# An encoder layer on one core: input loads one step later, grouped exponentials, weight sums at half rate, four buffers for values

## The chip, the core and the metric

The kernel runs on one core of one Trainium2 chip. The metric is the device time of one execution in microseconds (us); the kernel before has a median of 2715.44 us over three runs (2715.1 to 2720.17).

The engines are TensorE (PE in the profile, its weight loads PEld), VectorE (DVE), ScalarE (ACT), GpSimd (POOL) and SyncE (SP). SP, ACT and POOL also issue DMAs. Each engine works through its own instructions in order: an instruction that waits holds all that stand behind it, and an instruction that issues a DMA waits like any other.

## The reference

One bidirectional encoder layer with shared weights on 256 + 1024 tokens of width 1024, all in float32. Cut to the parts that this case touches:

```python
h = rmsnorm(x, g_mix_pre)
z = h @ w_in
rq, rk, rv, rg, pin, mq, gl = jnp.split(z, list(IN_SPLITS), axis=-1)
gates = jax.nn.sigmoid(gl).reshape(b, s, N_BRANCH, D_MODEL)
# retention: scores times a decay matrix exp(log_gamma * distance), per head
decay = jnp.where(mask[None], jnp.exp(log_gamma[:, None, None] * jnp.maximum(diff, 0.0)[None]), 0.0)
y_ret = retention_branch(rq, rk, rv, rg, decay_fwd, decay_bwd, ret_gn) @ w_ret_out
# pooling: four groups of 256 channels, windows 2, 4, 8, 16
mean = (csg[:, hi] - csg[:, lo]) / (hi - lo)[None, :, None]
outs.append(mean - pf[:, :, sl])          # then a 256x256 product per group
y_pool = pool_branch(pin, pool_w, pool_scale) @ w_pool_out
# memory attention: keys and values from a normalised memory
kv = rmsnorm(mem, g_mem) @ w_mem_kv
y_mem = memory_branch(mq, mem, g_mem, w_mem_kv) @ w_mem_out
merged = gates[:, :, 0] * y_ret + gates[:, :, 1] * y_pool + gates[:, :, 2] * y_mem
x = x + rmsnorm(merged @ w_o, g_mix_post)
x = x + rmsnorm(conv_ffn(rmsnorm(x, g_ffn_pre), w_up, conv_w, conv_b, w_down), g_ffn_post)
```

## The kernel before

Every product is made of three matmuls of rounded halves (mm3): operands are split into a high part by ACT and a rest by DVE (hilo, and split_to for weights). Weights come as units of 128 x 1024: SP loads a unit into one of two raw buffers wr, ACT makes wh, DVE makes wl, into a ring of four; a raw buffer is loaded again when its split is issued, and a ring slot is free when PE is done with the unit four before. The order of all instructions on all engines is that of the Python code (a manual schedule). Small background generators in the list bg are advanced by one step at each call of tick(), after the weight split and the sum steps of that tick.

The stages in order, with the steps that the change touches:

- Memory keys: eight units m, each 24 matmuls; from m = 4 on DVE scales two finished banks per unit into tiles st (pool st0, three buffers) which POOL stores to km. In the background x_stats normalises x (loads by POOL, squares on ACT, scaling and hilo of eight hT tiles).
- Memory values: token_major with four weight units held and four token tiles in four PSUM banks (mm), twice (p = 0, 1). After the last unit mem_v evicts each bank on ACT into a tile st of the same three buffers, and ACT issues its store to vm.
- Value projection: token_major over ten token tiles, in blocks of 4, 1, 1 and 4 tiles, twice; v_out evicts into vst (two buffers) and ACT stores to vd. There are ten ticks per half. In the background in_terms loads eight chunks xs of x transposed on ACT's queue (three buffers), scales them on DVE and writes the sums and differences T1 to T4, two hilo's a step.
- Quads: twelve groups of four weight units (u0, s12, s34, a2), 7-product scheme; s12 and s34 are sums of weights that were formed in DRAM.
- Keys with rotary, memory attention, gates, then pooling and decay tables, states, retention, merge, output and the MLP. The MLP uses 22 more quads with formed sums.

The sums are made by DMA alone: sums() gives, for each of 34 quads, five steps: two plain copies issued by ACT (step 0) and four accumulating DMAs issued by POOL (steps 1 to 4), each on what an earlier step wrote. Step i of quad q is given out in round q + lag * i. sum_step() takes one step; tick() takes adding[0] of them: 1 in the memory values, 2 in the value projection, 1 later; each release of a weight unit in the quads takes one too. A load of s12 or s34 whose sum is not finished in this order takes all missing steps first.

pool_chain runs in the background of nine gate units (27 ticks). Per window: split the 256x256 weights into pwh, then for each of two channel tiles add shifted copies of an input tile pin on DVE, subtract, hilo into dh (one tick each), one empty tick, then two ticks of products evicted by ACT into ypo (two buffers), which POOL stores. load(m) takes a pin buffer, clears three edges with POOL memsets and loads two pieces on SP's queue. decay_matrix runs beside it and does one head per tick: two DVE operations, an Exp on ACT, a scaling on DVE. The gates use Sigmoid on ACT in between.

Of the kernel before, what the change touches and what calls it, by code (L numbers as in the profile page):

```python
# [17 lines left out]
P = 128  # L18
D = 1024
TP = 256  # L20
# [104 lines left out]
def encoder(ctx: ExitStack, tc: tile.TileContext, a: dict):  # L125
# [75 lines left out]
    summed = set()  # L201

    def sums():
        lag = 2

        def stage(i, q):
            u, v = (r.rearrange("p (a b) -> p a b", b=512) for r in sum_rows[q])
            both = lambda x: x.unsqueeze(1).to_broadcast([P, 2, 512])
            s12, s34 = s12_d[q], s34_d[q]
            if i == 0:  # L210
                nc.scalar.dma_start(out=s12[:], in_=both(v[:, 0, :]))
                nc.scalar.dma_start(out=s34[:], in_=u)
            elif i == 1:
                nc.gpsimd.dma_start(out=s12[:], in_=both(v[:, 1, :]), accum_op=ALU.add)
            elif i == 2:
                nc.gpsimd.dma_start(out=s34[:, 0, :], in_=v[:, 0, :], accum_op=ALU.add)
            elif i == 3:
                nc.gpsimd.dma_start(out=s12[:, 1, :], in_=u[:, 0, :], accum_op=ALU.add)
            else:
                nc.gpsimd.dma_start(out=s34[:, 1, :], in_=s12[:, 1, :], accum_op=ALU.add)  # L220
                summed.add(q)

        for n in range(len(sum_rows) + 4 * lag):
            for i in range(5):
                q = n - lag * i
                if 0 <= q < len(sum_rows):
                    stage(i, q)
                    yield
# [232 lines left out]
    def decay_matrix(pool):  # L461
        rel = pool.tile([P, 2, 2 * C], F32, name="rel")
        nc.sync.dma_start(out=rel, in_=a["rel"])
        yield
        for h in range(H):
            dt = dtab[:, h].rearrange("p a b -> p (a b)")
            nc.vector.tensor_scalar(out=dt, in0=rel[:, 0, :], scalar1=lg[:, h:h + 1], scalar2=None, op0=ALU.mult)
            nc.vector.scalar_tensor_tensor(out=dt, in0=rel[:, 1, :], scalar=lg[:, H + h:H + h + 1], in1=dt,
                                           op0=ALU.mult, op1=ALU.add)
            nc.scalar.activation(dt, dt, AF.Exp)  # L470
            nc.vector.tensor_scalar(out=dt, in0=dt, scalar1=HD ** -0.5, scalar2=None, op0=ALU.mult)
            yield

    def token_major(base, lhs, nt, out):
        blocks = [range(4)] if nt == 4 else [range(4), (4,), (5,), range(6, nt)]
# [19 lines left out]
    bg.append(mem_stats())  # L495
    bg.append(x_stats())
    bg.append(decay_tables())
    with tc.tile_pool(name="st0", bufs=3) as stp:
        done = []
        for m in range(8):  # L500
            (wh, wl), = ws.take()
# [16 lines left out]
                done = done[2:]  # L518
            tick()
        def mem_v(p, j, b):  # L520
            o = stp.tile([P, TM], F32, tag="st", name="st")
            nc.scalar.activation(o, b, AF.Copy, scale=mrs[:, j:j + 1])
            nc.scalar.dma_start(out=vm_d[p][:, j], in_=o[:].rearrange("p (a b) -> p a b", b=HD))

# [52 lines left out]

    def in_terms(pool):
        def load(c):
            t = pool.tile([P, TS], F32, tag="xs", name="xs", bufs=3)  # L580
            nc.scalar.dma_start(out=t, in_=a["xT"][:, c, TP:T])
            return t

# [4 lines left out]
        def put(nm, c, r):  # L588
            hilo(r, in_term(nm, c, 0), in_term(nm, c, 1))

        r1, r2 = load(0), load(4)
        yield
        for c in range(4):
            scaled(r1, c)
            if c < 3:
                n1 = load(c + 1)
            yield
            scaled(r2, c + 4)
            mix(r1[:, LO], r1[:, LO], r1[:, HI])
            put("T1", c, r1[:, LO])  # L600
# [4 lines left out]
            put("T2", c, r2[:, HI])  # L605
            mix(r2[:, LO], r2[:, HI], r2[:, LO], -1.0)
            put("T4", c, r2[:, LO])
            if c < 3:
                r1, r2 = n1, load(c + 5)
            yield  # L610

    with tc.tile_pool(name="vproj", bufs=1) as vp:
        def v_out(p, t, b):
            o = vp.tile([P, 512], F32, tag="vst", name="vst", bufs=2)
            nc.scalar.activation(o, b, AF.Copy)
            nc.scalar.dma_start(out=v_d[p][:, t], in_=o[:].rearrange("p (a b) -> p a b", b=HD))

        bg.append(in_terms(vp))
        adding[0] = 2
        token_major(v_at, hT, NT, v_out)  # L620
        drain()
    adding[0] = 1
# [2 lines left out]
    with tc.tile_pool(name="quads", bufs=1) as qp:  # L625
# [74 lines left out]
        for q in range(NQ):  # L700
            d, more = Q[q], q + 1 < NQ
            product(d["a"], unit("s12", q, 1), "T2", False, True)
            u2 = snap(qtile("u2", 2)[:], d["a"])
            pr(q, 0, 1)
            d["d"] = mmb(512)
            product(d["d"], unit("s34", q, 0), "T3", True, True)
            product(d["a"], unit("s12", q, 0), "T1", False, True)
# [194 lines left out]

    def pool_chain():
        pieces = ((PAD, 0, TP), (PAD + TP + PAD, TP, TS))
        pin = {}

        def load(m):
            if m < 2 * len(WINDOWS):
                t = pin[m] = pp.tile([P, PWA], F32, tag="pin", name="pin", bufs=2)
                for s in (0, PAD + TP, PW - PAD):  # L910
                    nc.gpsimd.memset(t[:, s:s + PAD], 0.0)
                for s, o, n in pieces:
                    nc.sync.dma_start(out=t[:, s:s + n], in_=pin_d[m // 2][:, m % 2, o:o + n])

# [11 lines left out]
        for g, w in enumerate(WINDOWS):  # L926
# [2 lines left out]
            load_w(g + 1)  # L929
            dh = []  # L930
            for c in range(2):
                x = pin.pop(2 * g + c)
                cur, lo, hi = x, PAD - 8, PW - PAD + 7
                step = 1
                while step < w:
# [25 lines left out]
                t = pp.tile([P, 2, PWA], F32R, tag="dh", name="dh", bufs=2)[:, :, 0:PCOLS]  # L961
                hilo(r, t[:, 0], t[:, 1])
                dh.append(t)
                load(2 * g + c + 2)
                yield
            yield
            for e in range(2):
                es = slice(e * P, (e + 1) * P)
# [986 lines left out]
```

## Time and profile before

| | |
|---|---|
| median of 3 runs | 2715.44 us |
| profiled execution | 2714.67 us |
| its span | 2712.9 us |
| PE busy | 2622.4 us (97%) |
| DVE, ACT, POOL busy | 1415.7, 982.7, 335.4 us |
| DMA, mean rate | 171 GB/s |

Busy time is the time in which an engine has an instruction running. What matters for the time is where PE has none: the list of waits gives for each engine and line the engine, tile and line that ended the wait, the sum in us, the count and the longest. In a timeline a row has start, duration, engine (ACTq and SPq are DMA issues), line, operation, output<-input and in brackets the idle time just before it and what ended it. The chain of waits is the list of work that ended last, followed back from the end.

### The profile page before, as it was taken

How to read it: one execution, taken by the hardware profiler on the slowest of the kernel's cores; microseconds unless marked ns; L12 is line 12 of the kernel's file. 1: busy time of each engine (PE TensorE's matmuls, PEld its weight loads, DVE VectorE, ACT ScalarE, POOL GpSimd, SP SyncE). 2: the span in 40 equal slices, each digit the busy share in tenths (PEclk: the TensorE clock that was granted, in tenths of full speed). 3: DMA queues.
4: the chain of work that ended last, by engine and by line, in shares of the span. 5: the costliest groups of instructions: out<-in, count | busy, mean ns of one | idle time of the engine just before them, and what ended most of it. 6: DMA issues, size and time to landing. Idle time of an engine off the chain costs nothing.

```text
span 2712.9 us, 35194 instructions
## 1 busy us (share of the span) xinstructions
PE 2622.4 (97%) x13580; PEld 2240.8 (83%) x13580; DVE 1415.7 (52%) x2343; ACT 982.7 (36%) x1637; POOL 335.4 (12%) x525
## 2 busy tenths in 40 slices
PE   8879999999988999999999999998999999999998
PEld 6668888889976788889888888877888888888886
DVE  4532323456624366688732444557666655664554
ACT  5322323324432233333321220466444444444443
POOL 1121222222222222111100000010000000000000
PEclk9889999999988999999999999999999999999999
DMA  7998777787667687555443442452333333354343
GB/s 270 310 267 223 209 213 217 211 245 196 186 165 213 170 225 205 191 177 185 147 170 121 132 148 88 159 194 88 112 111 113 113 108 115 113 183 153 143 158 109
DMA packets 181433, 464.88 MB, mean 171 GB/s; under 512 B 20721, under 2 KB 48241, under 8 KB 180721
## 3 DMA queue, kind: packets, MB, share of 16 engines
q1 hardware_dynamic: 111072, 268.33, 29.5%
q0 software_dynamic: 54384, 146.83, 21.0%
q10 hardware_dynamic: 15808, 47.47, 5.3%
q8 instruction: 106, 1.74, 0.2%
q14 instruction: 63, 0.51, 0.1%
HBM read 360.58 MB, written 182.19 MB: 200 GB/s over the span
## 4 chain that ended last, share of the span: by engine, by line
PE 83%; DMA 6%; DVE 5%; ACT 3%; issue 2%; POOL 0%; SPq 0%; ACTq 0%; DVEq 0%; POOLq 0%
PE f L1521 15%; PE f L164 10%; PE f L163 10%; PE f L162 10%; PE mm L639 7%; PE mm L162 6%; PE mm L163 6%; PE mm L164 6%; PE ch L163 3%; PE ch L164 3%; PE ch L162 3%; PE ch L639 1%; DMA wr<-w_kv_in 1%; DMA vm<-st 1%; DMA vd<-vst 1%
## 5 line engine op out<-in xcount | busy, mean ns | idle before, releaser
L90 DVE TENSOR_TENSOR wl<-wr,wh 128x1024 fp32r<-128x1024 f32 x268 | 327.5, 1224 | 516.1 <-ACT wh L89 511.2
L89 ACT ACTIVATE wh<-wr 128x1024 fp32r<-128x1024 f32 x268 | 280.7, 1051 | 269.1 <-PE f L163 150.6
L162 PE MATMUL mm<-b,wh 128*128 128x512 f32 (+1 forms) x960 | 342.6, 357 | 0.0
L163 PE MATMUL mm<-b,wh 128*128 128x512 f32 (+1 forms) x960 | 341.1, 355 | 0.0
L164 PE MATMUL mm<-b,wl 128*128 128x512 f32 (+1 forms) x960 | 340.5, 355 | 0.0
L1521 PE MATMUL f<-b,wh 128*128 128x512 f32 x880 | 273.8, 392 | 0.0
L164 PEld LDWEIGHTS mm<-b,wl 128*128 128x128 f32 x960 | 182.2, 190 | 25.7
L162 PEld LDWEIGHTS mm<-b,wh 128*128 128x128 f32 x960 | 182.5, 190 | 24.2
L163 PEld LDWEIGHTS mm<-b,wh 128*128 128x128 f32 x960 | 182.5, 190 | 23.6
L1521 PEld LDWEIGHTS f<-b,wh 128*128 128x128 f32 x880 | 162.0, 189 | 30.7
L1521 PE MATMUL f<-b,wl 128*128 128x512 f32 x440 | 171.9, 391 | 0.0
L163 PE MATMUL f<-b,wh 128*128 128x512 f32 (+1 forms) x432 | 153.4, 355 | 0.0
L162 PE MATMUL f<-b,wh 128*128 128x512 f32 (+1 forms) x432 | 153.1, 355 | 0.0
L164 PE MATMUL f<-b,wl 128*128 128x512 f32 (+1 forms) x432 | 152.8, 354 | 0.0
L164 PE MATMUL f<-wh,gl 128*128 128x512 f32 x390 | 151.8, 389 | 0.1
L162 PE MATMUL f<-wh,gl 128*128 128x512 f32 x390 | 151.8, 389 | 0.0
L163 PE MATMUL f<-wl,gl 128*128 128x512 f32 x390 | 151.7, 389 | 0.0
L155 DVE TENSOR_TENSOR gl<-b,gl 128x640 fp32r<-128x640 f32 x78 | 64.3, 825 | 118.2 <-ACT gl L154 116.9
L639 PE MATMUL mm<-T,wh 128*128 128x512 f32 x384 | 118.9, 391 | 0.5 <-ACT q L568 0.5
L154 ACT ACTIVATE gl<-b 128x640 fp32r<-128x640 f32 x78 | 57.5, 740 | 153.8 <-PE f L164 153.8
L1521 PE MATMUL f<-hc,wh 128*128 128x512 f32 x352 | 108.9, 391 | 0.0
L162 PE MATMUL f<-h2p,wh 128*128 128x256 f32 x352 | 100.0, 284 | 3.2 <-ACT h2p L154 3.2
(383 smaller groups left out, 5940.8 us busy)
## 6 DMA issues: line engine op xcount, KB each, us to landing
wr<-w_in_in SPq DMA_DIRECT2D x72, 512.0 KB, 5.3
wr<-w_up_in SPq DMA_DIRECT2D x44, 512.0 KB, 3.5
wr<-w_down_in SPq DMA_DIRECT2D x44, 512.0 KB, 3.5
wr<-s12d SPq DMA_DIRECT2D x34, 512.0 KB, 3.6
wr<-s34d SPq DMA_DIRECT2D x34, 512.0 KB, 3.5
b<-fgd SPq DMA_DIRECT2D x44, 320.0 KB, 5.2
h2s<-gtd SPq DMA_DIRECT2D x48, 256.0 KB, 3.7
s12d<-w_up_in ACTq DMA_DIRECT2D x22, 512.0 KB, 5.7
```

Source lines behind the costliest of these rows:

```text
L89: self.nc.scalar.activation(h, r[:], AF.Copy)
L90: self.nc.vector.tensor_tensor(out=l, in0=r[:], in1=h.bitcast(F32), op=ALU.subtract)
L154: nc.scalar.activation(hi, src, AF.Copy)
L155: nc.vector.tensor_tensor(out=lo, in0=src, in1=hi.bitcast(F32), op=ALU.subtract)
L162: nc.tensor.matmul(out, ah, bh, start=first, stop=False)
L163: nc.tensor.matmul(out, ah, bl, start=False, stop=False)
L164: nc.tensor.matmul(out, al, bh, start=False, stop=last)
L639: nc.tensor.matmul(b, w[x][:, ks], in_term(nm, c, y), start=first and c == k == 0, stop=last and c == 3 and k == 2, skip_group_check=True)
L1521: nc.tensor.matmul(b, w[x][:, ks], hterm(nm, c, y), start=first and c == k == 0, stop=last and c == 3 and k == 2, skip_group_check=True)
```

## The change

- sums(): lag is 1 instead of 2, so the five steps of a quad lie in consecutive rounds.
- The value projection takes one sum step per tick instead of two; each quad takes one more (five instead of four).
- decay_matrix: the heads' first two DVE operations still take one tick each, but all four Exps come in one tick after them, and all four scalings in the next.
- Pool st0: the tiles st for km have two buffers; mem_v uses tiles sv with four buffers of their own.
- in_terms: xs has two buffers instead of three; both loads of a chunk stand at the start of its turn, and the work starts two ticks later; a chunk takes four ticks instead of three.
- vst has four buffers instead of two.
- pool_chain: two lasting tiles pin0 and pin1, whose edges are cleared once at the start; a tile's next load is issued one tick later.

```diff
 def sums():
-        lag = 2
+        lag = 1
@@ decay_matrix
+        dt = [dtab[:, h].rearrange("p a b -> p (a b)") for h in range(H)]
         for h in range(H):
-            dt = dtab[:, h].rearrange("p a b -> p (a b)")
-            nc.vector.tensor_scalar(out=dt, in0=rel[:, 0, :], scalar1=lg[:, h:h + 1], ...)
-            nc.vector.scalar_tensor_tensor(out=dt, in0=rel[:, 1, :], scalar=lg[:, H + h:H + h + 1], in1=dt, ...)
-            nc.scalar.activation(dt, dt, AF.Exp)
-            nc.vector.tensor_scalar(out=dt, in0=dt, scalar1=HD ** -0.5, scalar2=None, op0=ALU.mult)
+            nc.vector.tensor_scalar(out=dt[h], in0=rel[:, 0, :], scalar1=lg[:, h:h + 1], ...)
+            nc.vector.scalar_tensor_tensor(out=dt[h], in0=rel[:, 1, :], scalar=lg[:, H + h:H + h + 1], in1=dt[h], ...)
             yield
+        for h in range(H):
+            nc.scalar.activation(dt[h], dt[h], AF.Exp)
+        yield
+        for h in range(H):
+            nc.vector.tensor_scalar(out=dt[h], in0=dt[h], scalar1=HD ** -0.5, scalar2=None, op0=ALU.mult)
@@ memory keys and values
-    with tc.tile_pool(name="st0", bufs=3) as stp:
+    with tc.tile_pool(name="st0", bufs=2) as stp:
...
         def mem_v(p, j, b):
-            o = stp.tile([P, TM], F32, tag="st", name="st")
+            o = stp.tile([P, TM], F32, tag="sv", name="sv", bufs=4)
@@ in_terms
-            t = pool.tile([P, TS], F32, tag="xs", name="xs", bufs=3)
+            t = pool.tile([P, TS], F32, tag="xs", name="xs", bufs=2)
...
-        r1, r2 = load(0), load(4)
-        yield
         for c in range(4):
+            r1, r2 = load(c), load(c + 4)
+            yield
+            yield
             scaled(r1, c)
-            if c < 3:
-                n1 = load(c + 1)
-            yield
             scaled(r2, c + 4)
...
-            if c < 3:
-                r1, r2 = n1, load(c + 5)
             yield
@@ value projection
-            o = vp.tile([P, 512], F32, tag="vst", name="vst", bufs=2)
+            o = vp.tile([P, 512], F32, tag="vst", name="vst", bufs=4)
...
-        adding[0] = 2
@@ quads
             pr(q, 0, 1)
+            sum_step()
             d["d"] = mmb(512)
@@ pool_chain
-        pin = {}
+        pin = [pp.tile([P, PWA], F32, name=f"pin{i}") for i in range(2)]
+        for t in pin:
+            for s in (0, PAD + TP, PW - PAD):
+                nc.gpsimd.memset(t[:, s:s + PAD], 0.0)
...
-                t = pin[m] = pp.tile([P, PWA], F32, tag="pin", name="pin", bufs=2)
-                for s in (0, PAD + TP, PW - PAD):
-                    nc.gpsimd.memset(t[:, s:s + PAD], 0.0)
+                t = pin[m % 2]
...
-                x = pin.pop(2 * g + c)
+                x = pin[c]
...
                 dh.append(t)
+                yield
                 load(2 * g + c + 2)
-                yield
             yield
```

## Rows read from the trace of the kernel before

**Rows 1.** The page: busy time, share of the span and instructions of each engine.
```profile
PE 2622.4 (97%) x13580; PEld 2240.8 (83%) x13580; DVE 1415.7 (52%) x2343; ACT 982.7 (36%) x1637; POOL 335.4 (12%) x525
```
**Rows 2.** Waits of PE, whole span: us in total, times, longest.
```profile
PE ch L162 <- ACT dh L154: 23.6, 5, 7.7
PE mm L162 <- ACT vst L615: 15.3, 3, 13.2
PE mm L162 <- ACT st L522: 13.3, 4, 5.4
```
**Rows 3.** Timeline of PE, 86 to 252 us: three starts.
```profile
86.72 0.80 PE L162 MATMUL mm<-wh,memT 128*128 128x512 f32 x1 [4.04 <-ACT st L522]
...
192.23 0.80 PE L162 MATMUL mm<-wh,b 128*128 128x512 f32 x1 [13.23 <-ACT vst L615]
...
251.92 0.62 PE L639 MATMUL mm<-b,wh 128*128 128x512 f32 x2
```
**Rows 4.** Chain of waits, first 900 us (start, us, what): one piece of 24 matmuls.
```profile
265.42 5.47 PE mm L639 x24
```
**Rows 5.** Table by stretches: us, then busy of five engines, PEclk, DMA share, GB/s.
```profile
185.00:190.00 5.00, 0.00 (x0) 0.00 (x0) 3.29 (x4) 1.61 (x2) 0.00 (x0) 0.50 1.08 311
```
**Rows 6.** Timeline of ACT, 80 to 130 us: a fourth eviction.
```profile
95.05 0.69 ACT L522 ACTIVATE st<-mm,rsy 128x512 f32<-128x512 f32 x1 [6.03 <-DMA vm<-st]
```
**Rows 7.** Timeline of DVE, 54 to 64 us: tiles st for km.
```profile
54.84 0.69 DVE L516 TENSOR_TENSOR st<-ch,mrb 128x512 f32<-128x512 f32 x1 [4.62 <-DMA km<-st]
...
59.93 0.69 DVE L516 TENSOR_TENSOR st<-ch,mrb 128x512 f32<-128x512 f32 x1 [2.66 <-DMA km<-st]
```
**Rows 8.** Chain of waits, 50 to 100 us (start, us, what).
```profile
57.56 5.45 DMA km<-st
...
63.75 1.22 DVE wl L90
64.99 8.42 DMA wr<-w_kv_in
```
**Rows 9.** Timelines of ACT and of DVE, 184 to 192 us.
```profile
184.93 1.06 ACT L89 ACTIVATE wh<-wr 128x1024 fp32r<-128x1024 f32 x1 [6.11 <-DMA wr<-w_in_in]
...
189.07 0.63 ACT L154 ACTIVATE T<-xs 128x512 fp32r<-128x512 f32 x1 [3.09 <-DVE xs L557]
191.06 0.63 ACT L154 ACTIVATE T<-xs 128x512 fp32r<-128x512 f32 x1 [1.36 <-DVE xs L557]
...
187.16 1.28 DVE L585 SCALAR_TENSOR_TENSOR xs<-xs,pk,xrb 128x1024 f32<-128x1024 f32 x1
```
**Rows 10.** DMA issues (last column median landing), and wr's tile view to 270 us.
```profile
xs<-xT_in ACTq DMA_DIRECT2D x8, 512.0 KB, 9.2
...
DMA to landing us min/median/max: 3.4/7.3/10.2
```
**Rows 11.** Timelines of ACT and of DVE, 775 to 815 us.
```profile
775.16 1.28 ACT L470 ACT_TABLE_LOAD   x1 [2.79 <-DVE dtab L468]
...
776.45 0.63 ACT L470 ACTIVATE dtab<-dtab 128x512 f32<-128x512 f32 x1
...
810.88 0.69 ACT L975 ACTIVATE ypo<-ch,pk 128x512 f32<-128x512 f32 x1 [5.03 <-DMA ypd<-ypo]
...
812.89 0.63 ACT L154 ACTIVATE pwh<-pwr 128x512 fp32r<-128x512 f32 x1
...
777.11 0.43 DVE L471 TENSOR_SCALAR dtab<-dtab 128x512 f32<-128x512 f32 x1 [2.02 <-ACT dtab L470]
```
**Rows 12.** Timeline of PE, 782 to 829 us: the second tile of two windows.
```profile
782.15 0.58 PE L162 MATMUL ch<-dh,pwh 128*128 128x256 f32 x1 [7.68 <-ACT dh L154]
...
828.96 0.58 PE L162 MATMUL ch<-dh,pwh 128*128 128x256 f32 x1 [5.46 <-ACT dh L154]
```
**Rows 13.** Timelines of SP and of PE in the quads: load and first use of a2.
```profile
423.08 7.18 SPq L73 DMA_DIRECT2D wr<-w_in_in  x2
...
437.98 0.28 PE L162 MATMUL ch<-b,wh 128*128 128x256 f32 x1
```

More of the change, by code (lines that the diff above doesn't have):

```diff
@@ L464, in decay_matrix @@
         yield
+        dt = [dtab[:, h].rearrange("p a b -> p (a b)") for h in range(H)]
         for h in range(H):
-            dt = dtab[:, h].rearrange("p a b -> p (a b)")
-            nc.vector.tensor_scalar(out=dt, in0=rel[:, 0, :], scalar1=lg[:, h:h + 1], scalar2=None, op0=ALU.mult)
-            nc.vector.scalar_tensor_tensor(out=dt, in0=rel[:, 1, :], scalar=lg[:, H + h:H + h + 1], in1=dt,
+            nc.vector.tensor_scalar(out=dt[h], in0=rel[:, 0, :], scalar1=lg[:, h:h + 1], scalar2=None, op0=ALU.mult)
+            nc.vector.scalar_tensor_tensor(out=dt[h], in0=rel[:, 1, :], scalar=lg[:, H + h:H + h + 1], in1=dt[h],
                                            op0=ALU.mult, op1=ALU.add)
-            nc.scalar.activation(dt, dt, AF.Exp)
-            nc.vector.tensor_scalar(out=dt, in0=dt, scalar1=HD ** -0.5, scalar2=None, op0=ALU.mult)
             yield
+        for h in range(H):
[3 more added lines that the diff above has]
+            nc.vector.tensor_scalar(out=dt[h], in0=dt[h], scalar1=HD ** -0.5, scalar2=None, op0=ALU.mult)
     def token_major(base, lhs, nt, out):
```

## The prediction

> **What bounds the kernel now.** The page first: TensorE (PE) is busy 97% of the span; its weight loads (PEld) run beside it, and every other engine is under 53% [rows 1]. So only what starves PE counts. The list of PE's waits names it: of all its waits three groups matter: 23.6 us in five waits for ACT's half of tile dh (the pooling branch), 15.3 us for the evictions into vst, 13.3 us for the evictions into st [rows 2]. All the rest is far smaller. The change touches the buffers behind all three, so I read the timelines of two stretches: 86 to 252 us (second half of the memory values, then the value projection) and 755 to 830 us (pooling).
>
> First stretch. Its work is 24 steps of 24 matmuls (4 tiles x 2 x 3, or 4 weights x 2 x 3): 4 steps for memory values, 20 for the projection. 24 such matmuls take 5.47 us at full clock [rows 4], so 24 x 5.47 = 131.3 us. PE starts at 86.72 and the next stage's first matmul is at 251.92: 165.2 us [rows 3]. Lost: 33.9 us. PE's gaps on st and vst are 28.6 us [rows 2], of which the 4.04 at 86.72 lies before the stretch; 24.6 lie in it. The other 9.3 us are matmuls at the lower clock: during such a gap the granted clock falls to 0.50 of full, that is 1.2 GHz [rows 5], and the first matmuls behind it are slow; I take four spells of about 2.3 us loss each.
>
> Why the gaps: ACT works in order. The fourth eviction of a half waits for a store of the same buffer to land: ACT stands 6.03 us at 95.05 for vm<-st [rows 6], and behind it stand the weight splits and the hT halves that PE needs. The big one, 13.23 us at 192.23 [rows 3], is a convoy on ACT: a split at 184.93 that waited 6.11 us for its weight DMA, then two halves of in_terms at 189.07 and 191.06, each waiting for DVE, which had just done its 1.28 us scaling at 187.16 [rows 9]; only behind them come the vst evictions that free PE's banks. The DMA engines are full there: share 1.08 [rows 5].
>
> **The change, part by part.**
>
> *Four buffers for the values (sv in mem_v, vst in v_out).* Each half has four tiles, so with four buffers no eviction of a half waits for a store of its own half. An eviction takes 0.69 us plus the issue, about 1.1 us. The four of the first memory half end some 5.5 us earlier, PE's second gap goes, the clock stays up, and the last step before the projection no longer stalls. What is late next is the hT chain of x_stats, which by my reading of the queues ends about level with PE: I leave 0.5 us of gap.
>
> *Later, fewer xs buffers.* A chunk's two loads are now issued after the chunk before is finished, then two ticks pass. A chunk then costs landing 9.2 us [rows 10], two scalings of 1.28 and four halves of 2.0 us each (189.07 to 191.06) [rows 9]: 9.2 + 2.6 + 8.0 = 19.8 us, against its four ticks, 4 x 5.47 = 21.9 us. It just fits. The steps fall differently: the evictions at the end of the first projection half now stand behind the loads of chunk 2 instead of behind a half-done chunk. Those loads sit on ACT and wait until DVE has finished the chunk before; I put their end 1.1 us behind PE (0 if the chunks land at 7 us, 8 if they take 15). Behind them on ACT: four evictions, then the next split, which PE needs some ten us later.
>
> The Trainium skill (DMA: Bandwidth & Descriptors, "Rules for kernel authors") speaks against this part: issue a DMA early and wait for it late. By that rule the loads would hold ACT; that case is the first rival below.
>
> *Sums at half rate, lag 1.* Counting the steps in the code: a sum is five steps; its last step is step 25 with lag 2 and step 15 with lag 1. Before, 8 steps run in the memory part and 40 in the projection; now 8 and 20. At the first load of an s12 (after the tenth projection tick) 17 steps will have run, 15 are needed; from there the margin is 7 steps, over one quad. So no load has to pull sums forward. At the end of the quads 88 of 170 steps are done instead of 96; the remaining 8 move into the later ticks, whose sums feed weights used only after 1100 us. A step that accumulates waits on POOL for the DMA six steps before it, 6 x 5.47 = 33 us: landed. What the quads carry is 5 steps instead of 4 in each. Cover: the tightest weight there is issued at 423.08 and used at 437.98, less its split 1.06 + 1.22 [rows 8, 9]: 12.6 us for its DMA [rows 13], while the slowest of the wr loads in the fullest stretch took 10.2 [rows 10]. So nothing, and the cost if the cover goes is the third rival.
>
> *The km tiles lose a buffer (st 3 to 2): a cost.* Eight tiles go out in four pairs. With three buffers DVE already waits 4.62 and 2.66 us for km stores [rows 7]. With two, each pair waits for the pair before: the first waits until 54.84 as now, pair 3 comes one landing later (54.84 + 0.7 + 0.3 + 5.45 = 61.3), pair 4 another (61.3 + 0.7 + 0.3 + 5.45 = 67.8, second tile done 69.2), landing 5.45 from the chain of waits [rows 8]. DVE's split at 63.75, which stands behind, slips 5.4 us; the weight load behind that split (8.42 us, only two raw buffers), the scaling of x and the eviction on which PE starts at 86.72 follow it in one chain [rows 8]. PE also stalls earlier, on the fourth bank, but inside the same slip. I take 5.4 us. Bounds: two landings at the fastest and slowest comparable DMA, 3.4 [rows 10] and 8.42 us [rows 8]: 1.3 to 11.3.
>
> Sum of the first stretch: it becomes 131.3 + 2.3 (the spell after 86.72 stays) + 0.5 + 1.1 = 135.2 us, 30.0 less; minus 5.4: 24.6 us.
>
> *Exponentials together.* Now each of the four heads makes ACT swap tables twice: 1.28 + 0.63 + 1.28 = 3.2 us, eight swaps; after it two [rows 11]. On the path: (a) DVE stands 2.02 us for the first Exp and then does 0.43 us of scaling [rows 11] before the second pooling tile, for which PE waits 7.68 us until 782.15 [rows 12]; both go: 2.4 us earlier. (b) The three other heads, 9.6 us, stand on ACT ahead of or among the ypo evictions of the first window; the last of these is at 810.88, and pwh of the next window at 812.89 comes behind it [rows 11]. After, these 9.6 us go, and one block of 2 x 1.28 + 4 x 0.63 = 5.1 us stands between the last eviction and pwh: pwh is 2.4 + 9.6 - 5.1 = 6.9 us earlier. DVE's four scalings, 1.7 us, now come between the window's two tiles: the second, for which PE waits until 828.96 [rows 12], is 5.2 us earlier. That is the whole gain of the stage (not 2.4 more); the later windows follow in chains of the same length. Bounds 2.4, only (a), and 6.9.
>
> First what the row shows: the swap takes 1.28 us and the Exp starts at 776.45, at once [rows 11]. The Trainium skill (ScalarE: Activation LUTs, "What ACT_TABLE_LOAD costs") gives 1283 ns and a drain of about 1380 ns more for each switch. By that figure, 2.66 us a switch, the gain of this part would be an estimated 11 us (2.4 + 17.9 - 7.8 - 1.7) instead of 5.2, and the time 2680; the trace shows no such drain, so the sum goes by the row.
>
> *Lasting pool inputs, loaded a tick later.* 18 memsets fewer on POOL, which waits there anyway; SP issues the two loads of a tile one tick later, behind that tick's weight load. The tile is used at least three ticks (16 us) on. Nothing; with that cover gone it would be one landing per tile, about 9 us, in front of dh.
>
> **Sum.** 24.6 + 5.2 = 29.8 us. The profiled execution took 2714.67 us (span 2712.9 plus 1.8 around it), the median of the runs is 2715.44. 2714.67 - 29.8 = 2684.9, against the median 2685.6. I say 2685.5.
>
> **Rivals.** (1) xs takes the place of vst: the chunks land late, ACT stands in front of their loads and the evictions wait as before. For: only 2 us of slack in 21.9, and the loads no longer run ahead. Against: half the sums are gone from that stretch. Then 13.2 of gap and one clock spell of 2.3 stay: 29.8 - 14.4 (1.1 is counted already) = 15.4, 2700 us. (2) It does not do what it says: the waits for landings only change their name, or the slip of km eats the rest (11.3 instead of 5.4, with rival 1): 2710 to 2715. (3) Slower: in the quads, weights land late because each quad carries a fifth step. Decides from a landing of 12.6 us; above it every quad loses the excess, 12 times. To turn the 29.8 us round it takes more than 15.1 us in every quad; at 17, 12 x 4.4 = 53 lost, 2738. Against: the slowest landing in a full stretch is 10.2.
>
> **How the numbers follow.** Forecast (2678 to 2693) 0.60; rival 1 (2693 to 2706) 0.22; still faster, by the fast ends of km and of part (b), 0.06; rival 2 0.07; rival 3 0.05. Range: fast end 29.8 + 4.1 (km) + 1.7 + 1.1 = 36.7, 2679; slow end as far as rival 1 with some of the km bound, 2704. A measurement of this kernel can tell about 0.2%, 5.4 us: faster 0.88, same 0.07, slower 0.05.
>
> **What would show it.** Right: PE's waits for sv and vst nearly gone; a new wait of DVE of 5 us or more for km at the third and fourth pair, PE's start of the second memory half at about 92; its 24 steps in 135 to 137 us; two table loads by the decay lines; second dh waits shortened by 5 us in sum with their stage; no PE wait in the quads. Wrong: a wait of 5 us or more for vst around 167 to 175 us (rival 1), a start of the second half later than 96 (km), PE waits for wl in the quads (rival 3), or g-window chains that take back what the Exps gave.

## The result, and the profile after

| | before | after |
|---|---|---|
| median of the runs | 2716.56 us (2715.1 to 2720.17, four runs) | 2693.37 us (2690.14 to 2694.28, four runs) |
| profiled execution, its span | 2714.67, 2712.9 us | 2693.02, 2691.0 us |

The ratio is 0.9911, 95% interval 0.9893 to 0.9928: 23.2 us faster. The prediction said 2685.5, range 2679 to 2704 (its forecast proper 2678 to 2693), and gave "faster" 0.88.

The engines' line of the page, to be read against [rows 1]:

```profile
PE 2620.8 (97%) x13580; PEld 2240.8 (83%) x13580; DVE 1414.4 (53%) x2343; ACT 974.7 (36%) x1631; POOL 335.4 (12%) x507
```

The list of PE's waits, against [rows 2] (us in all, times, longest us):

```profile
PE ch L162 <- ACT dh L154: 22.6, 5, 7.4
PE mm L162 <- ACT sv L525: 9.8, 2, 5.3
...
PE ch L163 <- DVE khl L155: 3.4, 1, 3.4
```

The 15.3 us on vst are gone, of the 13.3 on st 9.8 are left under the name sv, and the 23.6 on dh are 22.6. The timeline of PE gives the places, as [rows 3] did:

```profile
87.24 0.80 PE L162 MATMUL mm<-wh,memT 128*128 128x512 f32 x1 [4.47 <-ACT sv L525]
117.05 0.80 PE L162 MATMUL mm<-wh,b 128*128 128x512 f32 x1 [5.33 <-ACT sv L525]
228.85 0.61 PE L637 MATMUL mm<-b,wh 128*128 128x512 f32 x2
```

The second half of the memory values starts 0.5 us later than before, the first quad matmul comes 23.1 us earlier (251.92 before), and there is no gap over 0.4 us between 117.05 and 228.85: nothing in the place of the 13.23 at 192.23.

To see where the rest of the time goes I cut each span at five marks that all runs have: the first quad matmul; the last one (the quads take 298.3 or 298.4 us in every run with a change but e1, 298.8 there and 299.2 before); DVE's first product with cos in the key stage; DVE's first operation of pooling; PE's last gap on dh. All columns are us; the runs are those of the next section. The medians come from several chips, on which the kernel before has 2713.07 to 2716.56, so runs of different chips are compared by their ratio to it; e1 to e4 ran on one chip, e5 to e8 on a second, e9 to e12 on a third.

| kernel | first quad matmul | last quad to cos | last quad to pooling | pooling to last gap | from there to the end | span | median of runs |
|---|---|---|---|---|---|---|---|
| before | 251.9 | 16.7 | 216.0 | 148.8 | 1797.0 | 2712.9 | 2716.56 |
| after | 228.9 | 19.2 | 222.0 | 143.2 | 1798.6 | 2691.0 | 2693.37 |
| e8 after, again | 226.2 | 18.9 | 223.2 | 147.1 | 1798.9 | 2693.8 | 2693.04 |
| e1 values alone | 242.6 | 16.2 | 217.1 | 147.9 | 1796.6 | 2703.0 | 2702.96 |
| e9 sums alone | 241.6 | 19.0 | 223.1 | 145.9 | 1798.4 | 2707.2 | 2707.63 |
| e4 Exps alone | 253.8 | 17.4 | 219.3 | 141.0 | 1796.6 | 2709.1 | 2708.17 |
| e2 after, old sums | 237.5 | 16.2 | 215.6 | 141.7 | 1797.2 | 2690.3 | 2697.11 |
| e3 after, three st | 225.8 | 19.3 | 223.4 | 144.1 | 1797.8 | 2689.4 | 2692.32 |
| e5 after, 3 steps more | 228.9 | 16.9 | 216.7 | 141.1 | 1798.2 | 2683.2 | 2683.97 |
| e10 after, 5 steps more | 226.1 | 19.7 | 223.0 | 144.4 | 1796.8 | 2688.6 | 2690.01 |
| e6 after, quiet | 225.4 | 10.8 | 213.9 | 143.0 | 1802.8 | 2683.4 | 2687.47 |
| e7 after, five xr | 223.4 | 19.4 | 222.2 | 145.4 | 1799.4 | 2688.7 | 2690.16 |
| e11 e5 with e7 | 222.4 | 16.7 | 216.7 | 142.3 | 1800.1 | 2679.8 | 2682.64 |
| e12 e11, old pool inputs | 223.3 | 17.2 | 217.4 | 143.7 | 1799.0 | 2681.6 | 2682.96 |

The marks of one execution repeat only roughly: after and e8 are the same code and differ by 2.6 us at the first quad matmul and by 3.9 from pooling to the last gap, and e1 and e2, which are the same code up to the first quad matmul, differ by 5.0 there. So a row of this table is read with others beside it. Before to after: -23.1 (first quad matmul), -0.8 (quads), +6.0 (up to pooling), -5.6 (pooling), +1.6 (rest), in all -21.9, the difference of the spans. So the stretch did about what was said. Behind the quads the 5.2 us of the Exps were to come on top, and from the last quad matmul to the last gap the time went from 364.8 to 365.2 us (370.3 in e8): what pooling gained was lost ahead of it, where the prediction had nothing. The columns up to and from the start of pooling are best added up, since PE works on gates while pooling starts, and a late start may shorten the stage behind it.

### The profile page after: what moved, and what is told of

Read it like the earlier page. It is cut to its first block, busy times and chain, and to the rows that moved or that the text cites. A ratio compares the mean times of both kernels' runs of the same rounds, so it can differ in the third digit from the quotient of the medians.

```text
span 2691.0 us, 35137 instructions
## 1 busy us (share of the span) xinstructions
PE 2620.8 (97%) x13580; PEld 2240.8 (83%) x13580; DVE 1414.4 (53%) x2343; ACT 974.7 (36%) x1631; POOL 335.4 (12%) x507
## 4 chain that ended last, share of the span: by engine, by line
PE 80%; issue 7%; DVE 5%; DMA 4%; ACT 2%; POOL 1%; SPq 0%; DVEq 0%; ACTq 0%; POOLq 0%
PE f L1521 15%; PE f L164 10%; PE f L163 9%; PE f L162 9%; PE mm L637 7%; PE mm L162 6%; PE mm L163 6%; PE mm L164 6%; PE ch L163 3%; PE ch L164 3%; PE ch L162 3%; PE ch L637 1%; DMA ypd<-ypo 1%; DVE ps L944 1%; DMA qkvr<-vd 1%
## 5 line engine op out<-in xcount | busy, mean ns | idle before, releaser
L163 PEld LDWEIGHTS mm<-b,wh 128*128 128x128 f32 x960 | 182.4, 190 | 23.6
```

Source lines behind the costliest of these rows:

```text
L163: nc.tensor.matmul(out, ah, bl, start=False, stop=False)
```

## The experiments

**e1, e9 and e2: is it the buffers or the halved sums?** e1 is the kernel before with the value buffers alone: the diff below, and in_terms as in the kernel after (two buffers xs, both loads at the start of a chunk's turn):

```diff
-    with tc.tile_pool(name="st0", bufs=3) as stp:
+    with tc.tile_pool(name="st0", bufs=2) as stp:
...
-            o = stp.tile([P, TM], F32, tag="st", name="st")
+            o = stp.tile([P, TM], F32, tag="sv", name="sv", bufs=4)
...
-            o = vp.tile([P, 512], F32, tag="vst", name="vst", bufs=2)
+            o = vp.tile([P, 512], F32, tag="vst", name="vst", bufs=4)
```

> The kernel before with the value buffers alone (two tiles st, four sv, four vst, two xs loaded at the start of a chunk's turn); sums, Exps and pool inputs as before. Theory 'buffers': the stretch up to the first quad matmul shortens by the waits that the buffers remove, whatever the sums do: first quad matmul at 228 to 231 us (251.92 before, 228.85 after), no wait for vst over 2 us, time 2692 to 2697. Rival 'relief': the chunks of x land in time only because half of the sum steps are gone from the value projection (landing of xs 9.2 us before, 5.7 after); with two sum steps per tick they land at 9 us or more, ACT stands in front of their loads, and a PE wait of 8 us or more for vst stays around 170 to 195: first quad matmul at 238 or later, time 2702 or more.

Measured: 2702.96 us, ratio 0.9954 (0.9940 to 0.9969); first quad matmul at 242.55. The rival "relief" holds. From the timeline of e1, rows of ACT and its queue, DVE and PE in order of time:

```profile
157.90 1.08 ACTq L581 DMA_DIRECT2D xs<-xT_in  x2
...
170.36 1.28 DVE L585 SCALAR_TENSOR_TENSOR xs<-xs,pk,xrb 128x1024 f32<-128x1024 f32 x1 [7.95 <-DMA xs<-xT_in]
...
174.34 0.63 ACT L154 ACTIVATE T<-xs 128x512 fp32r<-128x512 f32 x1 [13.19 <-DVE xs L557]
...
183.48 1.10 ACTq L581 DMA_DIRECT2D xs<-xT_in  x2
184.63 0.60 ACT L611 ACTIVATE vst<-mm 128x512 f32<-128x512 f32 x1 [1.27 <-DVE wl L90]
...
185.28 0.80 PE L162 MATMUL mm<-wh,b 128*128 128x512 f32 x1 [10.73 <-ACT vst L611]
```

The chunk's loads, issued at 157.90, are there for DVE at 170.36, 12.5 us later. ACT stands 13.19 us for DVE, the next chunk's loads follow at 183.48, and the four evictions that free PE's banks come behind these: PE has stood for 10.73 us. That is the mechanism of the prediction's first rival, here with the sums at their old rate.

e9 is the other corner, the kernel before with only the sums changed:

```diff
-        lag = 2
+        lag = 1
...
-        adding[0] = 2
...
             pr(q, 0, 1)
+            sum_step()
```

> The kernel before with only the sums changed (lag 1, one step per tick in the value projection, one more in each quad); value buffers, Exps and pool inputs as before. Together with the value buffers alone (first quad matmul 242.55, 9.4 earlier than before) and the changed kernel (226 to 229) this closes a square. Theory 'both are needed': the vst waits with two buffers stay whatever the DMA does, since an eviction waits for a store of its own half; the halved sums alone shorten the 13.2 us wait by less than half: first quad matmul at 245 to 250, and the key stage loses its 2.5 to 3 us, the pooling its 2 to 6: time 2712 to 2720, no faster than before. Rival 'the sums did it': the halved sums alone bring 12 us or more: first quad matmul at 240 or earlier, time 2708 or less.

Measured: 2707.63 us, ratio 0.9981 (0.9971 to 0.9990); first quad matmul at 241.55, between the two expectations. The time, 5.4 us less than before, lies in the range of the second (2708 or less), against the first theory's "no faster". The loss of the key stage and up to pooling came much as the first theory said (19.0 and 223.1, 2.3 and 7.1 more than before; 2.5 to 3 and 2 to 6 were expected). ACT's timeline of e9 at the end of the first projection half:

```profile
178.82 0.60 ACT L615 ACTIVATE vst<-mm 128x512 f32<-128x512 f32 x1 [0.41 <-ACT vst L615]
179.45 0.33 ACTq L616 DMA_DIRECT2D vd<-vst  x1
186.43 0.60 ACT L615 ACTIVATE vst<-mm 128x512 f32<-128x512 f32 x1 [7.01 <-DMA vd<-vst]
```

Here the chunks are in time (median landing 4.9 us from 130 to 235 us), and what is left is the wait that two buffers make: the third eviction stands 7.01 us for the store of the first. PE waits less for it than in e1:

```profile
187.08 0.80 PE L162 MATMUL mm<-wh,b 128*128 128x512 f32 x1 [4.01 <-ACT vst L615]
```

With a first wait of 1.92 us at 178.47 that is 5.9 us, against 15.3 before [rows 2], 10.7 in e1 and none after. So two different waits stood in one place, and each part of the change takes away one of them. Alone they bring 9.4 us (e1; 14.4 in e2, the same code up to there) and 10.4 us (e9) at the first quad matmul; together 23.1 and 25.7 (after and e8). With marks that differ by 5 us between executions, these figures do not show that the two bring more together than the sum of each alone; what is shown is that each alone leaves a wait that the other removes. The stretch from 165 to 200 us in the list of windows (us, then busy time of PE, PEld, DVE, ACT and POOL with counts, granted clock, DMA share, GB/s), for before, e1, e9 and after, one fence each:

```profile
165.00:200.00 35.00, 20.06 (x77) 15.55 (x75) 15.12 (x18) 9.62 (x14) 10.73 (x12) 0.76 0.99 280
```
```profile
165.00:200.00 35.00, 24.27 (x96) 19.52 (x95) 14.59 (x16) 8.10 (x12) 10.73 (x12) 0.80 1.04 295
```
```profile
165.00:200.00 35.00, 29.08 (x108) 23.02 (x108) 17.51 (x21) 9.37 (x14) 3.58 (x4) 0.85 0.72 203
```
```profile
165.00:200.00 35.00, 35.00 (x156) 29.01 (x155) 16.44 (x21) 12.17 (x18) 5.47 (x6) 1.00 0.86 246
```

The last two numbers tell e1 from after: a DMA share of 1.04 against 0.86. And what a load then costs stands in the list of issues from 130 to 235 us (count, KB each, median us from issue to landing), e1 and then after:

```profile
xs<-xT_in ACTq DMA_DIRECT2D x8, 512.0 KB, 12.0
s34d<-s12d POOLq DMA_DIRECT2D x5, 256.0 KB, 15.7
```
```profile
xs<-xT_in ACTq DMA_DIRECT2D x8, 512.0 KB, 5.7
s34d<-s12d POOLq DMA_DIRECT2D x2, 256.0 KB, 13.7
```

e2 is the kernel after with the old sums (the diff of e9 backwards).

> The kernel after with the sums as before (lag 2, two steps per tick in the value projection, four per quad). The changed kernel loses some 6 us between the last quad matmul (527.16, 23.9 earlier than before) and the start of pooling on DVE (749.18, only 17.9 earlier). Theory 'phase': these 6 us come from which sum step meets which load there (88 instead of 96 steps done at that point); with the old count the start of pooling lies 22 to 24 us earlier than before if the value stretch keeps its gain, time 2686 to 2690. Theory 'neutral' (the prediction: the sums are worth nothing): first quad matmul within 1.5 us of 228.85, time within 2 us of the changed kernel's. Rival 'relief': the value stretch needs the halved sums: first quad matmul at 238 or later, time 2700 or more.

Measured: 2697.11 us, ratio 0.9933 (0.9917 to 0.9949). It bears out the core of "relief" and of "phase", though it falls short of the numbers of both (237.54 against 238 or later, 2697.11 against 2700 or more, and against 2686 to 2690): the value stretch needs the halved sums (first quad matmul 237.54, a vst gap of 11.33 at 181), and with the old sums the loss up to pooling is away (215.6). "Neutral", the prediction's own term, falls. In the profiled executions the two effects nearly cancel: the halved sums brought some 9 to 11 us up to the first quad matmul (237.5 against 228.9 and 226.2) and cost 8 to 13 us from the quads to the last pooling gap (357.3 against 365.2 and 370.3, the two columns up to and from the start of pooling added up). The profiled execution of e2 is its fastest (2692.04, median 2697.11), so its row flatters it by some 5 us; by the ratios the halved sums gain (0.9911 and 0.9919 against 0.9933), hardly clear of the noise.

**e5, e10 and e6: where the 6 us went.** The number of steps done when the quads end was 96 before and is 88 after, so other kinds of steps meet the later loads. A step of kind 0 moves two copies of 512 KB, kind 1 one of 512 KB, kinds 2 to 4 one of 256 KB each; under way they come in turn, so that five steps more are the same kind again. e5 does 91 steps, three more, so that the kinds stand as before:

```diff
-            sum_step()
+            sum_step(2 if q >= NQ - 3 else 1)
```

> The kernel after with one more sum step in each of the last three quads: 91 instead of 88 steps are done at the end of the quads, so that the same kinds of steps as before the change (next: an accumulating step of POOL, not the two plain copies on ACT) meet the loads of the key stage. Measured so far, from the last quad matmul to the first rotary product of DVE (which waits for cos): 16.7 us before, 16.2 in both runs with the old sums, 17.4 with the Exps alone, but 19.2 and 19.3 with the new sums; and to the start of pooling on DVE 216 to 220 against 222.6 and 224.0. Theory 'phase': which steps meet these loads decides; here 16 to 17.5 and 216 to 220, time 2687 to 2690. Rival 'early copies': it is having 8 steps fewer done (so more of them later), or chance; here 19 and 222 or more, time within 1.5 us of the changed kernel's.

Measured: 2683.97 us, ratio 0.9883 (0.9866 to 0.9899), 9.1 us less than the changed kernel on the same chip (e8, 2693.04). The time is below the theory's 2687 to 2690. Key stage 16.9, pooling after 216.7, pooling itself 141.1.

> The kernel after with one more sum step in each of the last five quads: 93 steps done at the end of the quads, five more than in the changed kernel, so the same kinds of steps meet the later loads as there. With three more (91) the time was 2683.97 against 2693.04, and pooling began 216.7 us after the last quad matmul against 222.0 and 223.2. Theory 'phase' (the kind of step): the loss is back, first rotary product 18.5 to 19.5 after the last quad matmul, start of pooling 221 to 224, time 2690 to 2694. Rival 'count' (more steps done early, fewer later): 16.5 to 17.5, 215 to 217.5, time 2682 to 2686.

e10 is that edit with `NQ - 5`: 93 steps, five more than after, so the same kinds as there. Measured: 2690.01 us, ratio 0.9919 (0.9904 to 0.9934), with 19.7 and 223.0: the loss is back, and the ratio is that of e8 (0.9919). Having more steps done is no cure; where the five kinds stand is what counts. All runs fall in line: 16.2 to 17.4 and 215.6 to 219.3 with the kinds of before (before, e1, e2, e4, e5, e11, e12), 18.9 to 19.7 and 222.0 to 223.4 with those of the changed kernel (after, e3, e7 to e10). The meeting itself, at the start of pooling, in the timeline of the changed kernel (ACT's queue, SP's, POOL's, then ACT):

```profile
732.64 0.56 ACTq L211 DMA_DIRECT2D s12d<-w_up_in  x1
733.23 0.63 ACTq L212 DMA_DIRECT2D s34d<-w_up_in  x1
...
735.89 3.70 SPq L913 DMA_DIRECT2D pin<-pind  x4
739.51 1.13 POOL L214 DMA_DIRECT2D s12d<-w_up_in  x1
...
739.76 0.33 SPq L921 DMA_DIRECT2D pwr<-pool_w_in  x1
...
748.52 0.63 ACT L154 ACTIVATE pwh<-pwr 128x512 fp32r<-128x512 f32 x1 [9.85 <-DMA pwr<-pool_w_in]
```

and in that of e5:

```profile
733.05 1.81 SPq L913 DMA_DIRECT2D pin<-pind  x4
735.02 0.39 SPq L921 DMA_DIRECT2D pwr<-pool_w_in  x1
...
743.26 0.63 ACT L154 ACTIVATE pwh<-pwr 128x512 fp32r<-128x512 f32 x1 [7.44 <-DMA pwr<-pool_w_in]
...
747.90 0.56 ACTq L211 DMA_DIRECT2D s12d<-w_up_in  x1
```

In the changed kernel the two plain copies go out just ahead of the loads of pin and a 512 KB addition beside that of pwr: SP's pin loads take 3.70 instead of 1.81 us to issue, and pwr is split 8.76 us behind its issue (748.52 - 739.76) instead of 8.24. In e5 the copies come only at 747.90, with the loads done. From the last quad matmul to the split of pwr it is 221.4 us against 216.0 in e5; of these 5.3 us, 2.9 are there before the pin loads, 1.9 come in their issue and 0.5 in the landing of pwr. e10 shows the bad case once more, in ACT's timeline, 9.83 us behind an issue at 736.95:

```profile
746.78 0.63 ACT L154 ACTIVATE pwh<-pwr 128x512 fp32r<-128x512 f32 x1 [10.76 <-DMA pwr<-pool_w_in]
```

e6 makes no step in the last quad, the first rotary unit, the memory gate and the first pooling gate; while still[0] is set, sum_step() does nothing:

```diff
+            still[0] = not more
...
         rotary_unit(k_d[h], mp, *cs_)
+        still[0] = False
+    still[0] = True
     for _ in range(N_MEM):
         gate_unit(mp)
...
         gate_unit(pp)
+        still[0] = False
```

> The kernel after with no sum steps in the last quad, in the first rotary unit, in the memory gate and in the first pooling gate (they are made up later). Theory 'the sums' DMAs delay the loads of cos, km and the pooling weights': from the last quad matmul to the first rotary product on DVE below 16 us (19.2 in the changed kernel; the load of cos then lands in 6 to 9 us instead of 13), the pooling weights land in 5 to 6 us instead of 8.75, pooling on DVE starts 6 to 10 us after the last quad matmul earlier than in the changed kernel (213 to 217 instead of 222.6), time 2683 to 2688. Rival 'not the sums' (the queue order of wr and cos on SP, or the store traffic): 19 and 222 stay, time within 1.5 us.

Measured: 2687.47 us, ratio 0.9897 (0.9883 to 0.9912). DVE's timeline:

```profile
534.51 0.69 DVE L861 TENSOR_TENSOR rt<-mm,cos 128x512 f32<-128x512 f32 x1 [6.62 <-DMA cos<-cos_in]
```

The load of cos was issued at 528.30: 6.2 us, against 13.0 in the changed kernel (533.38 to 546.40). So the sums' transfers are what makes that load late. By which of them the kinds cost the key stage its 2 to 3 us is open, though: in e5 the copies go out just ahead of the load of cos as well (530.14, the load at 533.32). A slow load of cos is not new either: from its issue to the product that uses it are 10.8 to 12.8 us in before, e1, e2, e4, e5, e11 and e12, and 11.4 to 13.7 in after, e3 and e7 to e10, where it is mostly issued later, too (5.3 to 8.3 us behind the last quad matmul, against 4.6 to 6.1). pwr is split 6.9 us behind its issue in e6 (expected 5 to 6). But of the 8 to 9 us gained up to pooling (213.9) some 4 are given back behind the last gap (1802.8): the steps left out have to be made later, and the rest of the kernel is longer. I did not follow where.

**e3: the buffer that the km tiles lost.** One word of the kernel after, `bufs=2` to `bufs=3` in st0.

> The kernel after with three tiles st for the memory keys instead of two. The prediction's term: the lost buffer makes the second half of the memory values start 5.4 us late; giving it back starts that half near 82 us instead of 87.24 and gains about 5 us of the time, 2688. Rival: the stores of km land at 3 to 6 us and the third and fourth pair wait 2.1 us each instead of one landing each, and the next weight's load ends the wait anyway: the half starts at 86 to 87, time within 1.5 us of the changed kernel's.

Measured: 2692.32 us, ratio 0.9921 (0.9906 to 0.9936). The rival holds; PE starts the second half at 86.45 instead of 87.24 (86.67 in e8):

```profile
86.45 0.50 PE L162 MATMUL mm<-wh,memT 128*128 128x512 f32 x1 [3.08 <-ACT sv L525]
```

The third buffer is worth 0.2 to 0.8 us by these, not 5.4; the spread is larger than that (e5, with two buffers and the same code up to there, starts at 89.04). DVE's timeline of after, the last km tiles, shows why; [rows 7] and [rows 8] are the same of before:

```profile
58.41 0.69 DVE L519 TENSOR_TENSOR st<-mm,mrb 128x512 f32<-128x512 f32 x1 [2.10 <-DMA km<-st]
61.20 0.69 DVE L519 TENSOR_TENSOR st<-ch,mrb 128x512 f32<-128x512 f32 x1 [2.10 <-DMA km<-st]
...
64.86 0.69 DVE L519 TENSOR_TENSOR st<-ch,mrb 128x512 f32<-128x512 f32 x1 [1.24 <-DMA km<-st]
65.47 1.22 DVE L90 TENSOR_TENSOR wl<-wr,wh 128x1024 fp32r<-128x1024 f32 x1
```

Of the last four tiles one does not wait at all (left out here) and three wait 1.24 to 2.10 us, not a landing of 5.45 us for each pair, since each store has been under way while DVE split the next weight. The split that stood at 63.75 is at 65.47, 1.7 us late, and the weight load behind it makes up for that: the split on ACT that waits for this load starts at 72.72, at 73.51 before.

**e4: the Exps alone**, the kernel before with the block of four Exps.

> The kernel before with the four decay Exps in one block and nothing else. Prediction: nothing moves up to 776 us, then 5.2 us are gained (2.4 before the second pooling tile, 4.5 less 1.7 plus nothing later): time 2710, second tile of window 2 ready for PE at about 779.7 and of window 4 at about 823.8. In the changed kernel that stage gained 7.0 measured from its own start on DVE. Theory 'all of it is the Exps': 7 us here too, 2708.5, window 4's second tile at 822. Rival 'half of it is other': the lasting pool inputs or the sums give 2 of the 7, and here it is 5 or less, 2710 or more.

Measured: 2708.17 us, ratio 0.9975 (0.9966 to 0.9985), 5.5 us less in the medians. Its pooling starts 3.3 us later after the quads than before (219.3), so the stage is read from its own start: to the second tile of window 2 12.6 us (15.0 before), to that of window 4 55.4 us (61.8 before), to the last gap 141.0 (148.8 before). So 2.4, 6.4 and 7.8 us. PE's timeline of e4, the second tiles of windows 2 and 4, against [rows 12]:

```profile
784.15 0.58 PE L162 MATMUL ch<-dh,pwh 128*128 128x256 f32 x1 [4.99 <-ACT dh L154]
...
826.92 0.58 PE L162 MATMUL ch<-dh,pwh 128*128 128x256 f32 x1 [7.09 <-ACT dh L154]
```

In this pair all of it is the Exps, but only the 2.4 repeats: to the second tile of window 2 every run with the block takes 12.6 or 12.7 us and every run without it 15.0. To that of window 4 the runs with the block take 54.9 to 58.0 us, those without it 61.8, 61.7 and 58.6 (before, e1, e9), and to the last gap 141.0 to 147.1 against 148.8, 147.9 and 145.9. It depends on the kinds of steps: from the last quad matmul to the last gap it is 364.8 and 365.0 without the block and 357.3 to 361.1 with it where the kinds are those of before, but 369.0 without (e9) and 365.2 to 370.3 with it where they are those of the changed kernel. So the Exps are worth some 6 us with the kinds of before, and in the changed kernel itself little of that can be seen.

**e7: one more tile for x transposed**, `bufs=4` to `bufs=5` for xr.

> The kernel after with five instead of four tiles for the loads of x transposed, so that each of the last loads is issued one tile (some 4 us) earlier. The prediction left 0.5 us of gap at the start of the value projection; measured were 5.33 us (at 117.05) and a spell at the lower clock, behind a last load that took 12.6 us. Theory 'hT is late because its last load is': the gap falls to 0.5 to 2 us, the first quad matmul comes 3.5 to 6 us earlier (223 to 225.5), time 2688 to 2690. Rival 'the transfers are bandwidth-bound (DMA share 1.0 from 90 to 135)': an earlier issue only lengthens the landings, the gap stays at 4 us or more and the first quad matmul within 1.5 us of 228.85.

Measured: 2690.16 us, ratio 0.9906 (0.9891 to 0.9920), 2.9 us less than e8; first quad matmul 223.37:

```profile
112.84 0.50 PE L162 MATMUL mm<-wh,b 128*128 128x512 f32 x1 [3.65 <-ACT sv L525]
```

The gap is smaller (5.33 and 4.41 in the two runs of the changed kernel) but not gone, and its end, 112.84, is 2.8 us earlier than in e8. The last load was part of it; DVE no longer waits for it (2.71 us in the changed kernel at 113.54), and what is left ahead of the evictions is DVE's and ACT's hT work.

> The changed kernel once more, unedited, beside these runs: what repeats of its marks. Expected of all theories: first quad matmul 228.85 within 1.5 us, gap at 117 of 4.5 to 6 us, from the last quad matmul to the first rotary product 19.2 within 0.5, to the start of pooling 222 to 224, time 2690 to 2695.

e8: 2693.04 us, ratio 0.9919 (0.9904 to 0.9934). The time repeats; the first quad matmul (226.23) was 2.6 us off the first profile, more than I had allowed, and the gap, 4.41 at 115.68, is a little under the 4.5 expected.

**e11 and e12.** e11 has the edits of e5 and e7, e12 is e11 with the pool inputs as before the change (buffers in turn, edges cleared at each load, loads a tick earlier).

> The kernel after with three more sum steps in the last quads (91) and five tiles for x transposed. If the two gains are independent (9.1 us and 2.9 us): first quad matmul at 222 to 225, pooling 216 to 217.5 after the last quad matmul, time 2679.5 to 2682.5. Rival: the values' gain of 3 us is lost again before the pooling, whose start is set by landings: 2683 to 2685.

> The same kernel as the third of this call, but with the pool inputs as before the change: buffers taken in turn, their edges cleared by POOL at each load, the next load a tick earlier. The prediction's term is nothing: time within 1.5 us of that run and its pooling windows of the same length. Rival: the 18 clearings on POOL stand between stores and cost or the earlier loads on SP meet the weights: 2 us or more in one direction, visible in the time from the start of pooling to its last PE gap (143.2 and 147.1 us in the changed kernel, 148.8 before).

e11: 2682.64 us, ratio 0.9894 (0.9878 to 0.9911). Not told apart: it lies between the two expectations, and by the ratios it is no better than e5. e12: 2682.96 us, ratio 0.9894 (0.9880 to 0.9909): the pool inputs are worth nothing, as predicted.

## Why the prediction was right, and which terms were wrong

The prediction took 29.8 us off a profiled 2714.67; between the spans 21.9 came. Its main mechanism held: the evictions' waits for their own stores went, the chunks came in time, and the Exps moved where it said. That the stretch came within 1.5 us of its term is luck, since two mis-sized terms cancel there and the halved sums, priced at nothing, carried part of it. By its own terms:

- *First stretch, 24.6:* 23.1. The start of the second half was put at 92.1 (86.72 + 5.4) and came at 87.24, 4.9 better; its length was put at 135.2 and was 141.6 (228.85 - 87.24), 6.4 worse.
- *The slip for km, 5.4:* mis-sized, 0.2 to 0.8 (e3). The step that failed is "one landing later" for each pair: a landing counts from the issue, and most of it ran beside DVE's other work.
- *0.5 us for the hT chain:* mis-sized, 5.33 (4.41 in e8), and behind it a second spell at the lower clock, where the prediction had kept one. From 112 to 125 us, where the gap lies, the clock was 0.74 on the mean, that is partly at 1.2 GHz; the first matmul behind the gap took 0.80 us. That is the 6.4: 4.8 of gap, 2.7 at the lower clock (of the 141.6 us, 131.3 are work and 5.3 the gap, which leaves 5.0 where the prediction had 2.3), less the 1.1 for xs that did not come. "By my reading of the queues level with PE" rested on no row.
- *xs just fits:* right, but for a reason that the prediction had only named against its rival. It took the landing of before, 9.2 us, with a margin of 2.1 us; landings were 5.7 (after) with half the sums and 12.0 (e1) without. The Trainium skill's rule to issue a DMA early and wait late (DMA: Bandwidth & Descriptors, "Rules for kernel authors") fits what e1 shows, where ACT stood 13.19 us for a chunk, though no run changes the time of issue alone; in the changed kernel, at a share of 0.86, the late issue cost PE nothing.
- *Sums, nothing:* wrong twice, with opposite signs. The prediction counted only whether each sum is made in time and whether the quads bear a fifth step, and both held (no PE wait for a weight in the quads, 298.3 us: the third rival falls). It did not price what the steps do to other transfers: some 9 to 16 us gained up to the first quad matmul (e2 and e1 against after and e8), and some 9 lost behind the quads (e5 against e8, in time). "The remaining 8 move into the later ticks" is the sentence that failed: it asked when their results are needed, not what they meet.
- *Exps, 5.2 (2.4 to 6.9):* right in place and mechanism. (a) is 2.4 to the digit (e4: 15.0 to 12.6). The whole, 5.2 by the sum of (a), (b) and the scalings, is 6.4 to window 4 and 7.8 to the last gap in e4; in the changed kernel the loss ahead of pooling takes it back. The sign that the second dh waits would be 5 us shorter holds for window 2 alone (7.68 to 5.02); that of window 4 and the last one grew (5.46 to 7.09, 5.00 to 7.45), and all dh waits fell by only 1.0. ACT's timeline of after, against [rows 11]:

```profile
780.41 1.28 ACT L472 ACT_TABLE_LOAD   x1
781.70 2.19 ACT L472 ACTIVATE dtab<-dtab 128x512 f32<-128x512 f32 x4
783.91 1.28 ACT L869 ACT_TABLE_LOAD   x1
```

  One block of 4.8 us. The Exps start 0.01 us behind the end of the table load; the drain of about 1380 ns that the Trainium skill (ScalarE: Activation LUTs, "What ACT_TABLE_LOAD costs") adds to a switch doesn't show in this trace, and the 11 us that would follow from it did not come.
- *Pool inputs, nothing:* right (e12).

The forecast's centre was 8 us too fast chiefly because the loss behind the quads had no term; its range held it because the first rival's price had been taken in.

## What to carry to other kernels

Background DMA that is free of dependencies is not free: ask what each of its transfers will stand beside, above all where a stage opens with loads that nothing hides. When a gap has two causes in one place, one that waits for a store and one for a load, removing either leaves the other; try the corners of the square before giving the gain to one. A change of how many background steps run ahead shifts every later meeting of step and load, and three steps more were worth 9.1 us here, five more nothing by the ratio.

## What the runs showed of the hardware

- From a DMA share of 0.86 to one of 1.04 (165 to 200 us, after and e1) the rate rose from 246 to 295 GB/s, by a fifth, but the median landing of the 512 KB loads in that stage (130 to 235 us) from 5.7 to 12.0 us.
- An accumulating DMA within DRAM of 256 KB (s34d from s12d) landed in 13.7 us where a plain load of 512 KB took 5.7, and in 15.7 us in e1.
- Against the 13.0 us of the cos load in the changed kernel stand 6.2 in e6, with no sum step near it; in the other runs named there, with steps around it, 10.8 to 13.7 us passed from the issue to the first use.
